# Two more seven-product chunks per layer, combined in PSUM with ScalarE copies, and input sums taken from the transposes' banks

## The chip, the cores and the metric

The kernel runs on one core of one Trainium2 chip. The engines that matter are TensorE (PE in the profile; PEld is its weight load), VectorE (DVE), ScalarE (ACT) and GpSimd (POOL, which also issues some DMAs); SyncE (SP) issues the others. PE writes only into PSUM, which has eight banks of 128 partitions by 512 fp32 numbers; DVE and ACT read and write PSUM and SBUF. The metric is the device time of one execution in microseconds (us), the median of three runs.

## What is computed

A trunk of two layers over a residual stream `h` of 512 positions by 1024 features: an attention mixer (a different one in each layer), and after each a gated feed-forward part with a causal convolution of width 3. The change touches only the feed-forward part, whose reference is:

```
def conv_ffn(xn, w_up, cw, cb, w_down):
    a = xn @ w_up                      # 512 x 1024 @ 1024 x 5632
    ap = pad(a, 2 positions in front)
    a = sum(ap[:, j:j + T] * cw[j] for j in range(3)) + cb
    gate, val = split(a, 2)            # 2816 columns each
    return (gelu(gate) * val) @ w_down # 2816 x 1024
h = h + rms_norm(mixer, g[1])
h = h + rms_norm(conv_ffn(rms_norm(h, g[2]), ...), g[3])
```

All of it is fp32. The kernel writes each factor of a matrix product as a high and a low part in PE's reduced-precision fp32 (`hi` = the rounded copy, `lo` = the value less `hi`), and makes one product from three matmuls: hi·hi, hi·lo, lo·hi (`mm3`, lines 278 to 280 before, 292 to 294 after the change; these lines are those of nearly all matmuls).

## The kernel before, in words

**Tiling.** The up-projection of a layer goes in 22 chunks. Chunk `c` is 128 gate columns and the 128 value columns that belong to them, for all 512 positions: two PSUM banks, `banks[0]` for the gate and `banks[1]` for the value, each [128 columns, 512 positions]. A bank has two halves by position, LO (0 to 255) and HI (256 to 511).

**Plain chunks** (0 to 4 and 19 to 21): for each bank 8 steps over the 1024 features, 3 matmuls of 128x512 each: 48 matmuls. Chunks 0 and 1 are woven into the end of the mixer (`first_products`).

**Seven-product chunks** (5 to 18): the two column blocks, two halves of the features and two halves of the positions make a 2x2 by 2x2 block product, which is done with seven products in place of eight (Strassen's scheme in Winograd's form). Each product has 4 steps of 3 matmuls of 128x256, so a chunk has 84 of them. The seven products need sums of weight blocks and of input blocks, and sums of the results:

- The input sums (T1 to T4, as `xsh`/`xsl` pairs in XA and XB) are made once a layer in `sums_in` (lines 671 to 690): two additions that rebuild x from its parts, one on POOL (line 675) and one on DVE, four subtractions and four splits.
- The weight sums are made for each chunk in `first_weights` and `other_weights` (lines 699 to 733), each step placed by hand among the other work with `step` and `prepare`.
- The results are combined in the chunk's banks: one ACT copy of the first product out of PSUM (`s1`, line 1020), two DVE additions into SBUF (`s12`, `s17`, lines 998 and 1001) and three in PSUM (lines 1014, 1015, 1028).

**After the products**, `taps` (lines 636 to 649) does the convolution: one ACT operation a bank and two DVE operations a bank, then `glu` (ACT, Gelu) and `product` (POOL, a multiply and a DMA of the result to HBM). The taps of chunk c run during chunk c+1.

**Weights.** `Weights` hands out raw tiles of 512 KB, loaded by SP. A pair is made by an ACT copy (hi) and then either a DVE subtraction (`low`, line 69), or an ACT copy with its sign turned and a DMA of POOL's queue that adds the raw tile onto it (`low_added`, an accumulating DMA, with no DVE work).

**The boundary ahead of the layer's chunks.** `Boundary` takes the mixer's result block by block (128 positions each): `Mix.half` squares and scales it, `norm` makes the normalised block `xn` (ACT square at line 285, ACT square root, DVE `xn` at line 295), and `transpose` has PE transpose it into two banks (`xt_ps`, line 344), from which ACT makes `xbh` (line 347) and DVE `xbl` (line 348). These run between the mixer's last matmuls and `first_products`.

**What sets the order.** The program's order on each engine is as the code is written; every engine runs its list in that order. Waits between engines are semaphore counts that the framework places from the tiles that instructions read and write. A bank of PSUM is one tile here.

Of the kernel before, what the change touches and what calls it, by code (L numbers as in the profile page):

```python
# [16 lines left out]
T = 512  # L17
# [10 lines left out]
SEVEN = (5, 6, 7, 8, 9, 10, 11, 12, 13, 14, 15, 16, 17, 18)  # L28
# [7 lines left out]
class Weights:  # L36
# [3 lines left out]
    def __init__(self, nc, new_raw, new_pair, pieces):  # L40
        self.nc, self.new_raw, self.new_pair, self.pieces = nc, new_raw, new_pair, pieces
        self.ahead, self.ahead_dma = 4, 2
        self.raw, self.ready, self.half_done = {}, {}, []
        self.kept = {}
        self.n_dma = self.n_split = self.n_get = 0
# [48 lines left out]
    def split(self, n):  # L94
        while self.n_split < min(n, len(self.pieces)):
            self.high()
# [9 lines left out]
def trunk_kernel(ctx, tc, x, norm_gains, w_qkv_a, w_o_a, w_q_b, w_o_b, kv_norm, w_kvf, b_f,  # L106
# [63 lines left out]

    dT = [tc.dram_tile([ND, 128, 2048], F32, name=f"dT{l}") for l in range(2)]

    def add_ffn(l):
        for c in range(NF):
            add_cols(w_up[l], c * 128)
            add_cols(w_up[l], DFF + c * 128)
# [41 lines left out]
    W.kept = {v0: None, v0 + 1: None}  # L218

# [119 lines left out]
    def transpose_in(b, xn, xT):  # L339

        for i in range(2):
            pt = bank([128, 4, 128], name="xt_ps")
            for k in range(4):
# [4 lines left out]
            dve.tensor_tensor(lo[:, :, s], pt, hi[:, :, s].bitcast(F32), ALU.subtract)  # L348

# [62 lines left out]
    class Boundary:  # L412
# [218 lines left out]
    def ffn(l, bd, cp, nxt, ahead):  # L631
# [4 lines left out]
        def taps(c, banks, between=None):  # L636
            bb = t4([128, 2, T], name="bb")
            for s, ch in ((0, c), (1, NF + c)):
                ps = banks[s]
                act.activation(bb[:, s, :], ps, AF.Identity, bias=cp[:, 3, ch:ch + 1], scale=cp[:, 2, ch:ch + 1])  # L640
                dve.scalar_tensor_tensor(bb[:, s, 1:], ps[:, :T - 1], cp[:, 1, ch:ch + 1], bb[:, s, 1:],
                                         ALU.mult, ALU.add)
                dve.scalar_tensor_tensor(bb[:, s, 2:], ps[:, :T - 2], cp[:, 0, ch:ch + 1], bb[:, s, 2:],
                                         ALU.mult, ALU.add)
                if s == 0 and between is not None:
# [25 lines left out]
        def sums_in():  # L671

            v = [t8([128, 4, T], name=f"xsum{i}") for i in range(2)]
            for i, eng in enumerate((pool, dve)):
                eng.tensor_tensor(v[i], xT[0][i].bitcast(F32), xT[1][i].bitcast(F32), ALU.add)
            yield
            dve.tensor_tensor(v[0][:, :, LO], v[0][:, :, HI], v[0][:, :, LO], ALU.subtract)
            dve.tensor_tensor(v[0][:, :, HI], v[1][:, :, HI], v[0][:, :, HI], ALU.subtract)
            yield
            dve.tensor_tensor(v[1][:, :, HI], v[1][:, :, HI], v[0][:, :, LO], ALU.subtract)  # L680
            dve.tensor_tensor(v[1][:, :, LO], v[1][:, :, LO], v[1][:, :, HI], ALU.subtract)
            yield
            for X, src in ((XA, v[0]), (XB, v[1])):
                X += [t8([128, 4, T], F32R, name="xsh"), t8([128, 4, T], F32R, name="xsl")]
                for k in (0, 2):
                    act.copy(X[0][:, k:k + 2], src[:, k:k + 2])
                    dve.tensor_tensor(X[1][:, k:k + 2], src[:, k:k + 2], X[0][:, k:k + 2].bitcast(F32), ALU.subtract)
# [4 lines left out]
        def split_pair(pair, src, n=1024):  # L692
            act.copy(pair[:, 0, :n], src)
            yield
            dve.tensor_tensor(pair[:, 1, :n], src, pair[:, 0, :n].bitcast(F32), ALU.subtract)

        half_way = {}

        def first_weights(c):

            r0, r1 = W.take(2)
            w0, w1 = (t8([128, 2, 1024], F32R, name="w") for _ in range(2))
# [1263 lines left out]
```

## Time and profile before

The median of three runs is 1098.94 us (1098.63 to 1099.54). The profiled execution has a span of 1096.9 us from the first to the last instruction; 2.0 us of the median lie outside it.

| engine | busy us | share | instructions |
|---|---|---|---|
| PE | 1088.0 | 99% | 6896 |
| PEld | 956.4 | 87% | 6896 |
| DVE | 923.2 | 84% | 1534 |
| ACT | 687.4 | 63% | 1164 |
| POOL | 299.8 | 27% | 393 |

Where the layers lie in the span (from the start of the matmuls of each stage):

| stage | layer 0 | layer 1 |
|---|---|---|
| first products (chunks 0, 1) | 177.05 | 754.36 |
| chunks 2 to 4 (plain) | 201.80 | 779.11 |
| chunks 5 to 18 (seven products) | 234.47 | 811.78 |

How to read it: the profile's lines give a line of the code, the engine, the operation, the tile written and the tiles read, and times in us. A matmul's listed duration is longer than the distance to the next one, since matmuls are pipelined; the distance between starts is what it costs PE.

### The profile page before, as it was taken

The numbers are of one execution on the slowest core, as the hardware profiler recorded it, in microseconds if no ns is written. First come the engines' busy times: TensorE is split into PE (matmuls) and PEld (weight loads), VectorE is DVE, ScalarE is ACT, GpSimd is POOL, SyncE is SP. The second block draws the span as 40 slices with busy tenths as digits, with TensorE's granted clock in tenths as the row PEclk, the third lists the DMA queues.
The fourth block names the chain that finished last, engine by engine and source line by source line (L and its number), as shares of the span: only waits on it lengthen the run. The fifth ranks groups of instructions, "written<-read, shape, count | busy, mean of one in ns | idle before, by whom it ended". The sixth has DMA issues, their size and how long they took to land.

```text
span 1096.9 us, 19014 instructions
## 1 busy us (share of the span) xinstructions
PE 1088.0 (99%) x6896; PEld 956.4 (87%) x6896; DVE 923.2 (84%) x1534; ACT 687.4 (63%) x1164; POOL 299.8 (27%) x393
## 2 busy tenths in 40 slices
PE   9999999999999999999999999999999999999997
PEld 6988889899999988887988788789889999988886
DVE  6677778989999799897877877958989999799994
ACT  6644565567767547576565677756567677547572
POOL 4632101223233232000010667600223333231000
PEclk9999999999999999999999999999999999999999
DMA  9579854478999999794872777574378989999872
GB/s 315 141 272 407 334 154 137 106 153 205 214 205 211 267 339 345 275 327 95 212 154 77 213 230 202 164 235 130 92 164 200 211 205 212 270 339 339 291 249 77
DMA packets 188102, 240.52 MB, mean 219 GB/s; under 512 B 12193, under 2 KB 131993, under 8 KB 187497
## 3 DMA queue, kind: packets, MB, share of 16 engines
q1 hardware_dynamic: 167848, 177.66, 50.2%
q0 software_dynamic: 20160, 61.65, 25.2%
q8 instruction: 54, 0.88, 0.3%
q14 instruction: 40, 0.32, 0.1%
HBM read 170.28 MB, written 39.63 MB: 191 GB/s over the span
## 4 chain that ended last, share of the span: by engine, by line
PE 87%; issue 6%; DMA 2%; ACT 2%; DVE 1%; POOL 1%; SPq 0%; DVEq 0%; POOLq 0%; ACTq 0%
PE up L279 13%; PE up L278 13%; PE up L280 13%; PE acc L278 8%; PE acc L280 8%; PE acc L279 8%; PE qk_ps L1299 2%; PE o_ps L1818 2%; PE pT_ps L1803 2%; PE first L278 1%; PE first L280 1%; PE first L279 1%; PE qk_ps L278 1%; PE s_ps L1771 1%; PE qk_ps L280 1%
## 5 line engine op out<-in xcount | busy, mean ns | idle before, releaser
L278 PE MATMUL up<-xsh,w 128*128 128x256 f32 x448 | 126.9, 283 | 0.0
L280 PE MATMUL up<-xsh,w 128*128 128x256 f32 x448 | 126.9, 283 | 0.0
L279 PE MATMUL up<-xsl,w 128*128 128x256 f32 x448 | 126.9, 283 | 0.0
L278 PE MATMUL acc<-w 128*128 128x512 f32 (+1 forms) x311 | 120.6, 388 | 0.0
L280 PE MATMUL acc<-w 128*128 128x512 f32 (+1 forms) x311 | 120.4, 387 | 0.0
L640 ACT ACTIVATE bb<-up,conv 128x512 f32<-128x512 f32 x80 | 59.2, 775 | 92.3 <-DVE w L716 46.0
L279 PE MATMUL acc<-w 128*128 128x512 f32 (+1 forms) x267 | 103.3, 387 | 0.0
L69 DVE TENSOR_TENSOR w<-wraw,w 128x1024 fp32r<-128x1024 f32 x66 | 89.0, 1370 | 12.7 <-ACT w L60 12.3
L60 ACT CAST w<-wraw 128x1024 fp32r<-128x1024 f32 x80 | 82.3, 1050 | 9.3 <-issue 3.8
L280 PEld LDWEIGHTS up<-xsh,w 128*128 128x128 f32 x448 | 86.1, 192 | 0.0
L278 PEld LDWEIGHTS up<-xsh,w 128*128 128x128 f32 x448 | 86.1, 192 | 0.0
L279 PEld LDWEIGHTS up<-xsl,w 128*128 128x128 f32 x448 | 86.1, 192 | 0.0
L279 PE MATMUL up<-xcl,w 128*128 128x256 f32 (+1 forms) x264 | 85.0, 322 | 0.0
L279 PE MATMUL up<-xbl,w 128*128 128x256 f32 (+1 forms) x264 | 85.0, 322 | 0.0
L278 PE MATMUL up<-xbh,w 128*128 128x256 f32 (+1 forms) x264 | 85.0, 322 | 0.0
L278 PE MATMUL up<-xch,w 128*128 128x256 f32 (+1 forms) x264 | 85.0, 322 | 0.0
L280 PE MATMUL up<-xch,w 128*128 128x256 f32 (+1 forms) x264 | 85.0, 322 | 0.0
L280 PE MATMUL up<-xbh,w 128*128 128x256 f32 (+1 forms) x264 | 85.0, 322 | 0.0
L656 POOL TENSOR_TENSOR hc<-bb 128x512 f32<-128x512 f32 x44 | 68.6, 1559 | 27.0 <-ACT bb L661 13.6
L727 POOL DMA_DIRECT2D w<-wraw x28 | 24.0, 856 | 186.0 <-ACT w L726 178.8
L278 PEld LDWEIGHTS acc<-w 128*128 128x128 f32 x311 | 58.4, 188 | 11.9
L280 PEld LDWEIGHTS acc<-w 128*128 128x128 f32 x311 | 58.4, 188 | 11.8
(337 smaller groups left out, 3340.8 us busy)
## 6 DMA issues: line engine op xcount, KB each, us to landing
wraw<-in_w_up_dram SPq DMA_DIRECT2D x88, 512.0 KB, 6.4
w<-wraw POOLq DMA_DIRECT2D x42, 512.0 KB, 6.0
dT<-dsums SPq DMA_DIRECT2D x26, 512.0 KB, 4.1
hD<-hc POOLq DMA_DIRECT2D x44, 256.0 KB, 3.8
dact<-hD SPq DMA_DIRECT2D x44, 256.0 KB, 5.9
wraw<-dT SPq DMA_DIRECT2D x22, 512.0 KB, 6.8
wraw<-in_w_down_dram SPq DMA_DIRECT2D x22, 512.0 KB
dsums<-in_w_down_dram SPq DMA_DIRECT2D x18, 512.0 KB, 8.4
```

Of the source, the lines that this page charges most:

```text
L60: self.nc.scalar.copy(pair[:, 0, s], raw[:, s])
L69: self.nc.vector.tensor_tensor(pair[:, 1, s], raw[:, s], pair[:, 0, s].bitcast(F32), ALU.subtract)
L278: pe.matmul(o, ah, bh, start=first, stop=False, skip_group_check=shared)
L279: pe.matmul(o, ah, bl, start=False, stop=False, skip_group_check=shared)
L280: pe.matmul(o, al, bh, start=False, stop=last, skip_group_check=shared)
L640: act.activation(bb[:, s, :], ps, AF.Identity, bias=cp[:, 3, ch:ch + 1], scale=cp[:, 2, ch:ch + 1])
L656: pool.tensor_tensor(hc[c], bb[:, 0, :], bb[:, 1, :], ALU.mult)
L727: pool.dma_start(w3[:, 1, 0:512], a22, accum_op=ALU.add)
L1299: pe.matmul(o, ax(0, b, kc)[x], w[:, k, :], start=kc == 0 and x == 0 and w is wh, stop=kc == KD - 1 and w is wl)
L1771: pe.matmul(s[i][hh][:, :nn], q[a][rows, qs], k[b][rows, :nn], start=n == 0, stop=n == 2)
L1803: pe.transpose(o[:, k0 + k, :], p[:, hh, k * 128:(k + 1) * 128], ident)
L1818: pe.matmul(o[64 * hh:64 * hh + 64, i * 128:(i + 1) * 128], Vt[hd // 8][:, k, (hd % 8) * 64:(hd % 8) * 64 + 64], pT[j, i, hh][:, k, :], st ...
```

## The change

SEVEN becomes 3 to 18, so chunks 3 and 4 of each layer are made by seven products. Four things go with it.

1. *Combination.* A chunk's products come in the order S2, S3, A12, S1, then A11 of the next chunk, then A22, S4 (before: S2, S3, S1, A22, A11 of the next, A12, S4). Three ACT copies take results out of PSUM (`s1`, `u2`, `s7`; lines 999, 1023, 1028) and three DVE additions work in PSUM (lines 1035, 1038, 1049). The two additions into SBUF are gone.
2. *Weight sums.* `seven_weights` makes the blocks in another form: A11 as its own small pair (`wa`, 512 columns), A12 and A22 as one pair with one accumulating DMA, and the sums with a broadcast addition of 1024 columns (line 740) and two subtractions of 512 columns (lines 739, 745), two of them in place in the raw tile. Raw tiles are loaded by two DMAs of 256 KB.
3. *Input sums.* For blocks 0 and 1, ACT copies the transposes' banks into `xlow` (line 464). For blocks 2 and 3, DVE subtracts out of the banks (lines 468, 469). `sums` has two more DVE subtractions. `sums_in`, its POOL addition among it, is gone. `split_sums` makes the pairs.
4. *Taps and the first weights.* `taps` does the second bank first, and the DVE operations in another order. The weights of chunks 0 to 2 take the accumulating DMA in place of DVE's subtraction (`W.added`).

The core of the diff:

```diff
-SEVEN = (5, 6, 7, 8, 9, 10, 11, 12, 13, 14, 15, 16, 17, 18)
+SEVEN = tuple(range(3, 19))
...
     def split(self, n):
         while self.n_split < min(n, len(self.pieces)):
+            if self.n_split in self.added:
+                self.high_added()
+                continue
             self.high()
             self.low()
...
+    W.added = {n + i for n in starts for i in range(2 * SEVEN[0])}
...
         def transpose(self, b):
             if self.xT is None:
                 self.xT = new_xT(self.name)
-            transpose_in(b, self.xn.pop(b), self.xT)
+                self.low = t8([128, 2, 4, 256], name="xlow")
+            pts = transpose_in(b, self.xn.pop(b), self.xT)
+            s = slice(b % 2 * 128, b % 2 * 128 + 128)
+            if b < 2:
+                for i, pt in enumerate(pts):
+                    act.copy(self.low[:, i, :, s], pt)
+                return
+            if b == 2:
+                self.high = t8([128, 2, 4, 256], name="xsum")
+            dve.tensor_tensor(self.high[:, 0, :, s], pts[0], self.low[:, 0, :, s], ALU.subtract)
+            dve.tensor_tensor(self.high[:, 1, :, s], pts[1], self.high[:, 0, :, s], ALU.subtract)
...
+        def seven_weights(c):
+            r0, r1 = W.take(2)
+            a = t8([128, 2, 512], F32R, name="wa")
+            act.copy(a[:, 0], r0[:, 0:512])
             yield
+            act.activation(a[:, 1], r0[:, 0:512], AF.Copy, scale=-1.0)
+            pool.dma_start(a[:, 1], r0[:, 0:512], accum_op=ALU.add)
+            yield
+            b = t8([128, 2, 1024], F32R, name="w")
+            act.copy(b[:, 0], r1)
+            yield
+            act.activation(b[:, 1], r1, AF.Copy, scale=-1.0)
+            pool.dma_start(b[:, 1], r1, accum_op=ALU.add)
...
+            sb = t4([128, 1024], name="wsum")
+            dve.tensor_tensor(r0[:, 0:512], r0[:, 512:1024], r0[:, 0:512], ALU.subtract)
+            dve.tensor_tensor(sb.rearrange("p (q c) -> p q c", q=2), r0.rearrange("p (q c) -> p q c", q=2),
+                              r1[:, None, 512:1024].to_broadcast([128, 2, 512]), ALU.add)
+            u = t8([128, 2, 1024], F32R, name="w")
+            act.copy(u[:, 0], sb)
             yield
+            dve.tensor_tensor(r0[:, 512:1024], r1[:, 0:512], sb[:, 0:512], ALU.subtract)
+            v = t8([128, 2, 1024], F32R, name="w")
+            act.copy(v[:, 0], r0)
...
+            dve.tensor_tensor(u[:, 1], sb, u[:, 0].bitcast(F32), ALU.subtract)
...
+            dve.tensor_tensor(v[:, 1], r0, v[:, 0].bitcast(F32), ALU.subtract)
...
-                prod(o2, w["S2"], (*XB, HI))
-                prod(o3, w["S3"], (*XA, HI), True)
...
-                prod(o2, w["S1"], (*XA, LO))
-                prod(o3, w["A22"], (*XB, LO))
-                dve.tensor_tensor(o4, o2, s17, ALU.add)
-                dve.tensor_tensor(o3, o3, s12, ALU.add)
+                prod(o2, w.pop("S2"), (*XB, HI))
+                prod(o3, w.pop("S3"), (*XA, HI), True)
+                product()
+                bb = taps(*before)
...
+                act.copy(u2, o2)
...
+                prod(o1, w.pop("A12"), x21)
+                prod(o2, w.pop("S1"), (*XA, LO))
+                act.copy(s7, o3)
                 glu(before[0], bb)
...
+                dve.tensor_tensor(o1, o1, s1, ALU.add)
+                if m in SEVEN:
+                    step(m)
+                dve.tensor_tensor(o4, o2, s7, ALU.add)
+                if m in SEVEN:
+                    step(m)
+                    opened = open_seven(m)
...
-                prod(o1, w["A12"], x21)
-                prod(o2, w["S4"], x22)
+                prod(o3, w.pop("A22"), (*XB, LO))
                 prepare(c, 1)
+                dve.tensor_tensor(o3, o3, u2, ALU.add)
+                prod(o2, w.pop("S4"), x22)
                 prepare(c, 2)
-                dve.tensor_tensor(o2, o2, s1, ALU.add)
```

Here `o1`, `o2` are the LO and HI halves of `banks[0]`, `o3`, `o4` those of `banks[1]`; `m` is c+1 and `n` is c+2.

The order on PE in chunk 7 of layer 0 before, the first matmul of each product (`up_2725` and `up_2726` are the chunk's two banks, `up_2855` the first bank of chunk 8; `xsh` are the input sums, `xbh` the input itself; in brackets the engines whose counts the instruction waits for):

```order
L278 MATMUL up_2725<-xsh_2380,w_2548 128x256 [waits Activation_49]
...
L278 MATMUL up_2726<-xsh_2297,w_2548 128x256
...
L278 MATMUL up_2725<-xsh_2297,w_2712 128x256 [waits DVE_49,Activation_49]
...
L278 MATMUL up_2726<-xsh_2380,w_2713 128x256 [waits DVE_49]
...
L278 MATMUL up_2855<-xbh0_1854,w_2673 128x256
...
L278 MATMUL up_2725<-xbh1_1855,w_2547 128x256 [waits DVE_49]
...
L278 MATMUL up_2725<-xbh1_1855,w_2712 128x256
```

These are S2, S3, S1, A22, A11 of chunk 8, A12, S4. S1's DVE count is that of the addition at line 998, A22's that of line 1001, and A12's that of line 1014, which reads `up_2725`.

The same place of the changed kernel (`up_2854` and `up_2855` are the banks of chunk 7, `up_2984` the first of chunk 8):

```order
L292 MATMUL up_2854<-xsh_2265,w_2843 128x256 [waits Activation_49]
...
L292 MATMUL up_2855<-xsh_2290,w_2846 128x256 [waits PE_49]
...
L292 MATMUL up_2854<-xbh1_1859,w_2718 128x256 [waits Activation_49]
...
L292 MATMUL up_2854<-xsh_2290,w_2843 128x256
...
L292 MATMUL up_2984<-xbh0_1858,wa_2809 128x256
...
L292 MATMUL up_2855<-xsh_2265,w_2718 128x256 [waits DVE_49,Activation_49]
...
L292 MATMUL up_2854<-xbh1_1859,w_2846 128x256
```

These are S2, S3, A12, S1, A11 of chunk 8, A22, S4. S2 waits for the ACT copy `s1` (line 999), A12 for the ACT copy `u2` (line 1023). A22, which writes the LO half of `up_2855`, now waits for the ACT copy `s7` (line 1028) and for a DVE count that is that of line 1038, the addition `o4` into the HI half of `up_2855`.

The order on DVE in one chunk of the changed kernel, up to the next chunk's first weight sum:

```order
L739 TENSOR_TENSOR wraw<-wraw 128x512 [waits DMAHW1_49,DMAHW0_49,DMASW1_49]
L740 TENSOR_TENSOR wsum<-wraw 128x1024 [waits DMAHW3_49,DVE_49]
L745 TENSOR_TENSOR wraw<-wraw,wsum 128x512 [waits DMAHW2_49,DVE_49]
L1035 TENSOR_TENSOR up<-up,csum 128x256 [waits PE_49]
L752 TENSOR_TENSOR w<-wsum,w 128x1024 [waits DMASW4_49,Activation_49]
L1038 TENSOR_TENSOR up<-up,csum 128x256 [waits DVE_49]
L755 TENSOR_TENSOR w<-wraw,w 128x1024 [waits Activation_49]
L1049 TENSOR_TENSOR up<-up,csum 128x256 [waits DVE_49,PE_49]
L676 SCALAR_TENSOR_TENSOR bb<-up,conv,bb 128x511 [waits Activation_49] x2
L676 SCALAR_TENSOR_TENSOR bb<-up,conv,bb 128x510 [waits DVE_49] x2
```

The additions in PSUM are the rows `up<-up,csum`: `o1` (line 1035), `o4` (1038), `o3` (1049), with the low parts of the next chunk's weight sums (752, 755) between them. The wait of line 1035 on PE is for the last matmul of S1, which writes the other half of the same bank. Before, the additions of lines 1014 and 1015 stood back to back behind the taps.

The order on ACT at the boundary of the changed kernel, from block 0's transposes to the square of block 1's norm; before, line 299's square (285 there) came right behind the two casts:

```order
L363 CAST xbh_1858<-xt_ps 128x4x128 [waits PE_49]
L363 CAST xbh_1859<-xt_ps 128x4x128 [waits PE_49]
L464 COPY xlow<-xt_ps 128x4x128 [waits DVE_49] x2
L299 ACTIVATE junk,s_1879<-h 128x1024
L301 ACTIVATE sd<-s_1879,eps_t 128x1 [waits Activation_49]
```

The DVE count that the two copies wait for is that of the subtractions `xbl` (line 364) from the same two banks.

More of the change, by code (lines that the diff above doesn't have):

```diff
@@ L732, in other_weights @@
[L732 to L733 removed]
+            dve.tensor_tensor(u[:, 1], sb, u[:, 0].bitcast(F32), ALU.subtract)
+            del u, sb
+            yield
+            dve.tensor_tensor(v[:, 1], r0, v[:, 0].bitcast(F32), ALU.subtract)
         def plain_weights(c):
@@ L963, in ffn @@
         next(extra)
+        step(S0, 1)
         post(1, first[2:4])
+        del first
         next(extra)
-        W.ahead = 1
-        W.split(base + 8)
+        next(extra)
+        next(extra, None)
+        step(S0, 1)
         begun = opened = None
```

184 lines of the change are left out of this document (82 added, 102 removed).

## The prediction

> **What bounds the kernel now.** I read the page's busy shares first, then a table of windows over the up-projections, then the timelines of PE, DVE and ACT in one chunk.
>
> ```profile
> PE 1088.0 (99%) x6896; PEld 956.4 (87%) x6896; DVE 923.2 (84%) x1534; ACT 687.4 (63%) x1164; POOL 299.8 (27%) x393
> 234.00:435.00 201.00, 201.00 (x1441) 190.69 (x1440) 181.99 (x271) 132.33 (x176) 65.59 (x78) 1.00 0.93 248
> 812.00:1012.00 200.00, 200.00 (x1437) 189.85 (x1436) 181.45 (x270) 132.17 (x175) 65.69 (x78) 1.00 0.92 249
> 201.80:234.40 32.60, 32.60 (x146) 27.02 (x145) 30.17 (x33) 22.58 (x27) 8.01 (x9) 1.00 0.63 137
> ```
>
> The columns of the windows are span, then busy time of PE, PEld, DVE, ACT and POOL, the granted clock, the DMA share and GB/s. PE is busy for all of each window at a granted clock of 1.00: in the stage that is changed no engine ever keeps PE waiting. So PE's own work is the bound, less PE work is a gain one for one, and any new wait in PE's list is a loss one for one. DVE is the next engine (181.99 of 201 us): there is little slack to hide a late DVE operation.
>
> **What the change takes off PE.** A matmul costs the distance between starts:
>
> ```profile
> 203.19 0.39 PE L278 MATMUL up<-xbh,w 128*128 128x512 f32 x1
> ...
> 203.87 0.39 PE L278 MATMUL up<-xbh,w 128*128 128x512 f32 x1
> ...
> 334.90 0.28 PE L278 MATMUL up<-xbh,w 128*128 128x256 f32 x1
> ...
> 336.10 0.28 PE L279 MATMUL up<-xbl,w 128*128 128x256 f32 x1
> ```
>
> The first row stands three matmuls ahead of the second, the third ten ahead of the fourth: 0.68 / 3 = 0.2267 us for 512 columns, 1.20 / 10 = 0.120 for 256. A plain chunk is 48 x 0.2267 = 10.88 us, one of seven products 84 x 0.120 = 10.08. Two chunks more in each of two layers: 4 x 0.80 = **3.2 us less**. That is all the change can win, since DVE and ACT work that it removes (the POOL addition, two DVE additions a chunk) stands beside a PE that does not wait.
>
> **What it adds in each chunk: a wait of A22.** In the list of PE, A22 now waits for the DVE addition of line 1038 (`o4`), because both write the same bank, though different halves. In DVE's list `o4` stands behind `o1` (line 1035) and the low part of a weight sum (line 752), and `o1` waits for the last matmul of S1. On PE only A11 of the next chunk stands between S1 and A22. So I lay this chain end to end from rows of one chunk:
>
> ```profile
> 333.70 0.28 PE L280 MATMUL up<-xbh,w 128*128 128x256 f32 x1
> 334.02 0.37 ACT L1020 COPY csum<-up 128x256 f32<-128x256 f32 x1 [0.62 <-PE up L280]
> 336.91 0.42 DVE L1028 TENSOR_TENSOR up<-up,csum 128x256 f32<-128x256 f32 x1
> 337.25 1.22 DVE L716 TENSOR_TENSOR w<-wsum,w 128x1024 fp32r<-128x1024 f32 x1
> 338.38 0.42 DVE L998 TENSOR_TENSOR csum<-up,csum 128x256 f32<-128x256 f32 x1
> 215.04 0.75 DVE L643 SCALAR_TENSOR_TENSOR bb<-up,conv,bb 128x510 f32<-128x510 f32 x1
> 215.88 0.63 ACT L661 ACTIVATE bb<-bb 128x512 f32<-128x512 f32 x1 [2.19 <-DVE bb L643]
> ```
>
> From the start of a product's last matmul (333.70) to the start of the reader that waits for it (334.02) are 0.32 us. An addition in PSUM takes DVE 0.34 to the next start (336.91 to 337.25) and 0.42 to its end; a low part of 1024 columns takes 1.13 to the next start (337.25 to 338.38). From the end of a DVE operation (215.04 + 0.75 = 215.79) to an engine waiting for it are 0.09. With S1's first matmul at T: its last starts at T + 11 x 0.12 = T + 1.32; `o1` starts at T + 1.64; line 752 at T + 1.98; `o4` at T + 3.11, and ends at T + 3.53; A22 may start at T + 3.62. PE is ready for it at T + 2 x 12 x 0.12 = T + 2.88. **PE stalls 0.74 us in each chunk**, and the period goes from 10.08 to 10.82, nearly that of a plain chunk. The low part finds its high part ready: ACT has for one chunk about 7.5 us of work by the rows below, and stands idle before S1 ends. Chunk 18 is free of it: a plain chunk follows, no weight sum stands before `o4`, and the 12 matmuls of 512 columns that take A11's place last 2.72 us. So 15 chunks a layer, the first of which comes under the start-up; 2 x 14 x 0.74 = **20.7 us more**.
>
> DVE's own sum does not bind in this stage: per chunk the change needs two additions less and some 8.5 us by these rows. It is the place of one operation, not the load.
>
> ```profile
> L641 DVE SCALAR_TENSOR_TENSOR bb<-up,conv,bb 128x511 f32<-128x511 f32 x24 | 17.8, 742 | 0.8 <-DMA dsums<-in_w_down_dram 0.8
> L640 ACT ACTIVATE bb<-up,conv 128x512 f32<-128x512 f32 x22 | 16.2, 774 | 30.8 <-DVE w L716 11.5 <-PE up L280 10.5 <-DVE up L1028 8.8
> L729 ACT CAST w<-wsum 128x1024 fp32r<-128x1024 f32 x7 | 7.4, 1053 | 0.0
> L726 ACT ACTIVATE w<-wraw 128x512 fp32r<-128x512 f32 x7 | 4.4, 635 | 0.0
> ```
>
> [...]
>
> **What it adds at the boundary.** ACT's two copies into `xlow` for blocks 0 and 1 stand ahead of the next block's square, and each waits for the subtraction `xbl` from its bank.
>
> ```profile
> 167.88 1.07 ACT L347 CAST xbh<-xt_ps 128x512 fp32r<-128x512 f32 x2
> 168.82 1.08 ACT L285 ACTIVATE junk<-h 128x1024 bf16<-128x1024 f32 x1
> 168.73 1.28 DVE L348 TENSOR_TENSOR xbl<-xt_ps,xbh 128x512 fp32r<-128x512 f32 x2
> 170.55 1.42 DVE L295 SCALAR_TENSOR_TENSOR xn<-h,rs,gain 128x512 f32<-128x512 f32 x2
> 173.43 1.03 PE L344 MATMUL xt_ps<-ident,xn 128*128 128x128 f32 x8
> 175.02 1.28 DVE L348 TENSOR_TENSOR xbl<-xt_ps,xbh 128x512 fp32r<-128x512 f32 x2
> 176.89 1.42 DVE L295 SCALAR_TENSOR_TENSOR xn<-h,rs,gain 128x512 f32<-128x512 f32 x2
> 179.92 1.04 PE L344 MATMUL xt_ps<-ident,xn 128*128 128x128 f32 x8
> ```
>
> `xbl` ends at 170.01; the second copy runs from 170.1 for about 0.55 (half of the pair of casts). The square then starts at 170.55 or so, not at 168.82: 1.7 later, and `xn` ends at 171.97 + 1.7 = 173.67, where its transposes stood at 173.43. Stall 0.3 with the release. In the next round DVE's list has slipped by 1.7, its `xbl` by 1.2, and the copies take 1.7 again: `xn` ends 2.9 later, at 181.2, against 179.92 + 0.3: stall 1.0. Together **1.3 us a layer, 2.7 in all**. Bounds: 0 if the two copies hide in the 1.5 us between `xn` and its transposes, 2 a layer if DVE slips more.
>
> **What it adds at the start-up.** Chunk 3 is now the first of seven products, and its preparation stands at the place where chunks 0 and 1 have their taps. DVE's first weight sum (line 739) overwrites the raw tile, so it waits for the accumulating DMA that reads it.
>
> ```profile
> w<-wraw POOLq DMA_DIRECT2D x28, 256.0 KB, 3.7
> 188.14 1.06 ACT L60 CAST w<-wraw 128x1024 fp32r<-128x1024 f32 x1
> 193.43 0.78 ACT L640 ACTIVATE bb<-first,conv 128x512 f32<-128x512 f32 x1 [4.23 <-PE first L280]
> 197.99 1.28 ACT L661 ACT_TABLE_LOAD   x1 [0.97 <-DVE bb L643]
> 189.23 5.04 DVE L69 TENSOR_TENSOR w<-wraw,w 128x1024 fp32r<-128x1024 f32 x1
> 188.57 4.62 POOL L675 TENSOR_TENSOR xsum<-xbh,xbl 128x2048 f32<-128x2048 f32 x1 [51.77 <-DVE xbl L348]
> ```
>
> From 188.1 ACT makes the copies of a plain piece (1.05, 1.06) and those of A11 of chunk 3 (0.61, 0.64): 191.2. With 0.3 for the issue and 3.7 to 4 to land, line 739 starts at about 195.6. Now the engines wait for each other in turn: three DVE sums, ACT's highs of u and v (to 199.6) and of T2 (200.6), and only then the taps of chunk 0, which stood at 193.43. DVE's taps end at 204.5, the table load and Gelu at 206.4, T4's high at 207.3, its low at 209.2 (beside POOL's multiply: the row of 5.04 us, against 1.22, shows a DVE operation of two SBUF inputs held for as long as POOL's runs), u's low at 210.3, the taps of chunk 1 at 212.9, its Gelu at 213.6, T3's and T1's highs at 215.5, the lows of T3, T1 and v at 218.1. PE would start S2 of chunk 3 at 201.80 + 10.88 + 1.44 = 214.1. It waits there for ACT's copy `s1`, queued behind T1's high, until 215.9: 1.7 us; at S3 for v's low: 0.6; at A12 for the copy `u2`, which stands behind eight operations of ACT: 1.9; and at A22 for `o4`: 1.6. **5.6 us a layer** (5.8 with, 5.2 without the hold by POOL), and by 5.5 us to land 7.3; 11.2 in all. Below: some 3 if the queue's distances are shorter than I laid them.
>
> **What costs nothing.** The SP loads as two DMAs of 256 KB have a chunk of slack. The accumulating DMAs for chunks 0 to 2 take DVE work away and land some 10 us before PE needs them; uncovered, each would cost its 6.0 us of landing less what remains. The tail behind chunk 18 and the down-projection are as before.
>
> **Sum.** -3.2 + 20.7 + 2.7 + 11.2 = +31.4 us: a span of 1128.3, and with the 2.0 us that lie between the profiled span and the median of the runs, **1130 us**, 2.9% slower.
>
> **The rivals.** (1) *The waits are hidden and only PE's work counts*: 1098.9 - 3.2 = 1095.7, faster. For it: DVE is idle 8% of the stage, and a PSUM addition is short. Against it: the order of the lists is fixed, and `o4` would have to end 0.74 us earlier with its low part standing ahead. It decides if `o4` is done by T + 2.8. (2) *Only the start-up and boundary cost; A22's wait is met in the steady chunk*: 1098.9 - 3.2 + 13.9 = 1109.6. For it: the chain has only 0.74 us to lose, and the 1.13 of the low part is most of it. Against it: the four terms of the chain are measured at equal shapes. (3) *The waits go by halves*: then S4 is the one to wait for `o4`, 1.44 us later, the stall is gone, the `xlow` copies run beside `xbl`, and the start-up costs about 1 us a layer: 1098.9 - 3.2 + 2 = 1097.7, no change within what can be told. Against it: the program's counts. (4) *The loss feeds itself*: ACT's queue slips so that u's high or `u2` comes late in every chunk, or the landings of the accumulating DMAs (6.0 us median for 512 KB) reach A12's low matmul, at 0.3 to 1 us a chunk: 28 x 0.3 to 28 x 1 on top, 1139 to 1158. For it: DMAs are busy 93% of the stage; against it: PE's longer period gives them more room.
>
> **How the numbers follow.** The forecast has 0.63, its own range 1121 to 1139 (start-up from 3 to 7.3 and boundary from 0 to 2 a layer, the chunk from 0.6 to 0.8). Rival 2 has 0.13, rival 4 0.16, rival 1 0.05, rival 3 0.03. The range that leaves out 2 in 10 at most takes in the upper part of rival 2 and the lower of rival 4: 1110 to 1146. No change means within 0.2%, 2.2 us. Faster is rival 1 and a part of rival 3: 0.05; same 0.03; slower 0.92.
>
> **What would show it.** The distance from one chunk's first matmul to the next's is 10.8 us, with one gap of 0.7 ahead of A22's first matmul, released by DVE line 1038; a busy PE of 93% in the window of the chunks. In chunk 3 four gaps (S2, S3, A12, A22) with 5 to 6 us together; ahead of `first` two gaps at the transposes. DVE's `o1` starts 0.32 behind S1's last matmul. Wrong would be: no gap at A22, a gap in another place (S4, or A12 behind `u2` in every chunk), or a start-up over 8 us a layer.

## The result, and the profile after

The changed kernel takes 1144.24 us (median of four runs, 1144.14 to 1145.52), the one before 1098.79: 4.1% slower, ratio 1.0411 (95% interval 1.0397 to 1.0426). The profiled execution has a span of 1142.2 us, 45.3 more than before. The forecast was 1130: right in sign and in the place of the main loss, 14 us too low.

The page's busy shares, and two windows of layer 0 (span, then busy time of PE, PEld, DVE, ACT, POOL, the granted clock, DMA share, GB/s), the chunks from 4 on and the place of chunk 3:

```profile
PE 1098.7 (96%) x7040; PEld 964.8 (84%) x7040; DVE 878.4 (77%) x1468; ACT 735.8 (64%) x1264; POOL 301.6 (26%) x407
236.00:390.00 154.00, 144.95 (x1182) 142.36 (x1181) 123.12 (x169) 112.47 (x167) 49.48 (x56) 1.00 0.77 189
203.00:236.00 33.00, 28.13 (x170) 25.69 (x169) 23.80 (x30) 23.25 (x34) 8.38 (x9) 0.90 0.53 125
```

PE waits now in a stage where it never did: 9 of 154 us in the first window. DVE's busy time has fallen from 923.2 to 878.4 us, as the change meant, and experiment 8 shows that this is worth nothing. In the second window the granted clock is 0.90, where the windows of before that the prediction shows have 1.00.

One chunk of the steady stretch, first PE around A22 of one chunk and the start of the next one's, then DVE and ACT:

```profile
284.13 0.28 PE L294 MATMUL up<-xbh,wa 128*128 128x256 f32 x1
285.06 0.36 PE L292 MATMUL up<-xsh,w 128*128 128x256 f32 x1 [0.65 <-ACT w L729]
285.25 0.28 PE L293 MATMUL up<-xsl,w 128*128 128x256 f32 x1
296.00 0.36 PE L292 MATMUL up<-xsh,w 128*128 128x256 f32 x1 [0.65 <-ACT w L729]
283.01 0.43 DVE L1035 TENSOR_TENSOR up<-up,csum 128x256 f32<-128x256 f32 x1 [0.30 <-PE up L294]
283.36 1.22 DVE L752 TENSOR_TENSOR w<-wsum,w 128x1024 fp32r<-128x1024 f32 x1
284.49 0.43 DVE L1038 TENSOR_TENSOR up<-up,csum 128x256 f32<-128x256 f32 x1
283.93 1.04 ACT L729 CAST w<-wraw 128x1024 fp32r<-128x1024 f32 x1
```

The chain of the prediction stands there as it was laid: `o1` (L1035) behind S1, the low part (L752), `o4` (L1038) until 284.92, A22 at 285.06. A22 comes 0.93 us behind the matmul before it, not 0.12: a gap of 0.81. Its first matmul takes 0.19 to the next start (285.06 to 285.25), 0.07 more than the others. From one A22 to the next are 10.94 us here and 10.95 in the mean of chunks 4 to 17: 0.87 over the 84 x 0.120 = 10.08.

The profile names an ACT operation (L729, a weight copy for a later chunk) as what released A22. It ended at 284.97, by chance just behind `o4`; it is not what A22 needs. (At A22 of chunk 3, at 230.31, the profile names line 1038 itself.) The first experiment shows which it was.

The start of chunk 3, on PE, DVE and ACT, and the windows of what follows:

```profile
215.28 0.39 PE L294 MATMUL up<-xbh,w 128*128 128x512 f32 x1
219.29 0.58 PE L292 MATMUL up<-xsh,w 128*128 128x256 f32 x1 [3.62 <-ACT csum L999]
219.67 0.42 PE L293 MATMUL up<-xsl,w 128*128 128x256 f32 x1
219.89 0.41 PE L294 MATMUL up<-xsh,w 128*128 128x256 f32 x1
199.31 0.69 DVE L739 TENSOR_TENSOR wraw<-wraw 128x512 f32<-128x512 f32 x1 [5.17 <-issue]
218.88 0.36 ACT L999 COPY csum<-up 128x256 f32<-128x256 f32 x1
...
219.29:224.58 5.29, 5.29 (x24) 5.29 (x25) 3.96 (x5) 5.29 (x9) 2.96 (x4) 0.50 0.44 80
224.58:228.78 4.20, 4.20 (x36) 4.20 (x36) 4.08 (x7) 2.49 (x5) 1.44 (x3) 1.00 1.01 211
819.00:821.92 2.92, 2.92 (x13) 2.92 (x14) 2.25 (x2) 2.92 (x5) 0.87 (x1) 0.50 0.09 15
```

PE waits 3.8 us ahead of S2, not 1.7, and then runs at a granted clock of 0.50 for 5.29 us (24 matmuls, about 0.22 apart in place of 0.12) in layer 0 and for 2.92 us in layer 1. S3 and A12, which were to wait 0.6 and 1.9, come that much later in layer 0 and find their operands there; in layer 1, with 13 slow matmuls, A12 still waits for `u2`.

Two places more lose time where the forecast had none. Ahead of the down-projection's first products (`acc`):

```profile
431.43 0.39 PE L292 MATMUL acc<-w 128*128 128x512 f32 x1
433.52 0.50 PE L293 MATMUL acc<-w 128*128 128x512 f32 x1 [1.71 <-DVE w L815]
429.78 1.42 DVE L676 SCALAR_TENSOR_TENSOR bb<-up,conv,bb 128x511 f32<-128x511 f32 x2 [3.56 <-ACT bb L673]
431.12 1.21 DVE L815 TENSOR_TENSOR w<-dact,w 128x1024 fp32r<-128x1024 f32 x1
432.25 2.35 DVE L815 TENSOR_TENSOR w<-wraw,w 128x1024 fp32r<-128x1024 f32 x2
434.52 1.40 DVE L676 SCALAR_TENSOR_TENSOR bb<-up,conv,bb 128x510 f32<-128x510 f32 x2
```

and at chunks 18 and 19 (gaps of 0.2 and 0.6 us in layer 0), of which the second waits for a landing:

```profile
393.47 0.50 PE L294 MATMUL up<-xbh,w 128*128 128x512 f32 x1 [0.32 <-DMA w<-wraw]
```

From the starts of the matmuls of each stage, both kernels side by side, the 45.3 us go here (the stages outside the feed-forward parts differ by 0.5 us the other way):

| place | forecast, us | measured, us | from |
|---|---|---|---|
| PE's own work | -3.2 | -3.2 | counts and distances as before |
| A22, chunks 4 to 17, both layers | +20.7 | +24.4 | 28 x (10.95 - 10.08) |
| boundary, both layers | +2.7 | +1.9 | first products to chunk 2: 25.71 and 25.69, before 24.75 |
| start-up, chunk 3 | +11.2 | +15.5 | layer 0: 3.83 at S2, 2.41 of slow matmuls, 1.49 at A22; layer 1: 3.93, 1.37, 0.92 at A12, 1.60 at A22 |
| chunks 18 and 19 | 0 | +1.8 | gaps, with the longer first matmuls |
| start of the down-projection | 0 | +5.4 | to the next transposes: 103.36 and 103.37, before 100.65 and 100.64 |
| sum | +31.4 | +45.8 | |

### The profile page after: what moved, and what is told of

It is laid out like the page before. It is cut to its first block, busy times and chain, and to the rows that moved or that the text cites. A ratio compares the mean times of both kernels' runs of the same rounds, so it can differ in the third digit from the quotient of the medians.

```text
span 1142.2 us, 19621 instructions
## 1 busy us (share of the span) xinstructions
PE 1098.7 (96%) x7040; PEld 964.8 (84%) x7040; DVE 878.4 (77%) x1468; ACT 735.8 (64%) x1264; POOL 301.6 (26%) x407
## 4 chain that ended last, share of the span: by engine, by line
PE 64%; DVE 13%; ACT 12%; issue 7%; DMA 3%; POOL 0%; SPq 0%; DVEq 0%; ACTq 0%; POOLq 0%
PE acc L293 7%; PE acc L294 7%; PE acc L292 7%; PE up L292 5%; PE up L294 5%; PE up L293 4%; DVE bb L676 4%; DVE wsum L740 3%; ACT w L747 2%; ACT w L729 2%; PE v_ps L292 2%; PE v_ps L293 2%; PE v_ps L294 2%; ACT bb L673 2%; PE qk_ps L1325 2%
## 5 line engine op out<-in xcount | busy, mean ns | idle before, releaser
L292 PE MATMUL up<-xsh,w 128*128 128x256 f32 x512 | 149.2, 291 | 28.1 <-ACT w L729 16.8
L676 DVE SCALAR_TENSOR_TENSOR bb<-up,conv,bb 128x511 f32<-128x511 f32 (+1 forms) x160 | 112.0, 745 | 47.5 <-ACT bb L673 47.4
L293 PE MATMUL up<-xsl,w 128*128 128x256 f32 x512 | 146.3, 286 | 0.0
L294 PE MATMUL up<-xsh,w 128*128 128x256 f32 x512 | 146.3, 286 | 0.0
L292 PEld LDWEIGHTS up<-xsh,w 128*128 128x128 f32 x512 | 99.6, 195 | 34.5 <-ACT w L729 21.3
L293 PEld LDWEIGHTS up<-xsl,w 128*128 128x128 f32 x512 | 99.8, 195 | 0.1
L294 PEld LDWEIGHTS up<-xsh,w 128*128 128x128 f32 x512 | 99.7, 195 | 0.0
L673 ACT ACTIVATE bb<-up,conv 128x512 f32<-128x512 f32 x80 | 61.1, 777 | 55.4 <-DVE up L1049 41.1
L69 DVE TENSOR_TENSOR w<-wraw,w 128x1024 fp32r<-128x1024 f32 x50 | 61.5, 1246 | 14.1 <-ACT w L60 12.3
L292 PEld LDWEIGHTS acc<-w 128*128 128x128 f32 x311 | 58.4, 188 | 12.0
L294 PEld LDWEIGHTS acc<-w 128*128 128x128 f32 x311 | 58.4, 188 | 11.6
L293 PEld LDWEIGHTS acc<-w 128*128 128x128 f32 x267 | 50.1, 188 | 16.2 <-DVE w L815 6.2
L292 PE MATMUL up<-xch,w 128*128 128x256 f32 (+1 forms) x192 | 61.3, 319 | 0.7 <-ACT csum L1023 0.7
L294 PE MATMUL up<-xch,w 128*128 128x256 f32 (+1 forms) x192 | 61.2, 319 | 0.5 <-DMA w<-wraw 0.5
L743 ACT CAST w<-wsum 128x1024 fp32r<-128x1024 f32 x32 | 33.6, 1050 | 43.6 <-DVE wsum L740 43.6
L294 PE MATMUL up<-xbh,w 128*128 128x256 f32 (+1 forms) x192 | 61.2, 319 | 0.3 <-DMA w<-wraw 0.3
```

The costliest lines, as they stand in the source:

```text
L69: self.nc.vector.tensor_tensor(pair[:, 1, s], raw[:, s], pair[:, 0, s].bitcast(F32), ALU.subtract)
L292: pe.matmul(o, ah, bh, start=first, stop=False, skip_group_check=shared)
L293: pe.matmul(o, ah, bl, start=False, stop=False, skip_group_check=shared)
L294: pe.matmul(o, al, bh, start=False, stop=last, skip_group_check=shared)
L673: act.activation(bb[:, i, :], ps, AF.Identity, bias=cp[:, 3, ch:ch + 1], scale=cp[:, 2, ch:ch + 1])
L676: dve.scalar_tensor_tensor(bb[:, i, n:], ps[:, :T - n], cp[:, 2 - n, ch:ch + 1], bb[:, i, n:], ALU.mult, ALU.add)
```

## Experiments

### 1. Is it o4's place? Directly behind o1

```diff
                 dve.tensor_tensor(o1, o1, s1, ALU.add)
+                dve.tensor_tensor(o4, o2, s7, ALU.add)
                 if m in SEVEN:
                     step(m)
-                dve.tensor_tensor(o4, o2, s7, ALU.add)
```

> The addition o4 stands directly behind o1 in VectorE's list, ahead of the low part of the next chunk's weight sum; nothing else is changed. Theory (o4 is late only because the low part of 1024 columns stands ahead of it): o4 ends 1.13 us earlier, 0.3 us ahead of the time at which PE is ready for A22; the gap of 0.81 us ahead of A22 and the slower first matmul behind it are gone in chunks 4 to 17, the chunks come every 10.08 us, and 28 x 0.87 = 24 us go: 1120 us (1117 to 1123). Rival (A22 is held by something else in the chunk: ScalarE's copy s7, the weight pair that the released row names, or VectorE's load as a whole): the gap stays at 0.8 us and the time at 1144, within 3 us.

Measured: 1120.79 us (four runs, 1118.32 to 1123.45), ratio to before 1.0203 (1.0184 to 1.0223); 23.5 us less than the change by the medians. DVE, and the window of the same chunks:

```profile
280.45 0.43 DVE L1035 TENSOR_TENSOR up<-up,csum 128x256 f32<-128x256 f32 x1 [0.28 <-PE up L294]
280.99 0.43 DVE L1036 TENSOR_TENSOR up<-up,csum 128x256 f32<-128x256 f32 x1
281.33 1.22 DVE L752 TENSOR_TENSOR w<-wsum,w 128x1024 fp32r<-128x1024 f32 x1
...
232.00:370.00 138.00, 138.00 (x1152) 138.00 (x1151) 119.65 (x165) 107.95 (x164) 48.71 (x55) 1.00 0.85 209
```

PE is busy for all of 138 us: no gap is left in the steady chunks. The order of two DVE operations was worth the whole steady loss, and the ACT copy that the profile named as the releaser is where it was. By the starts of the matmuls in the two profiles, chunks 4 to 17 take 24.2 us less and chunk 3 takes 2.3 less; chunks 18 and 19 take 1.9 more, and the start of the down-projection 1.3 more, where eight matmuls of layer 0 run at the half clock. So a part of what was gained came back as longer waits further on, and the total meets the expected one partly because these cancel.

### 2. The other way: o4 behind both low parts

```diff
                 if m in SEVEN:
                     step(m)
-                dve.tensor_tensor(o4, o2, s7, ALU.add)
                 if m in SEVEN:
                     step(m)
+                dve.tensor_tensor(o4, o2, s7, ALU.add)
+                if m in SEVEN:
                     opened = open_seven(m)
```

> The addition o4 stands one operation further back, behind both low parts. Theory: the gap ahead of A22 grows by the 1.13 us that the second low part takes on VectorE, to 1.9 us, in every chunk from 3 to 17: 30 x 1.13 = 34 us more, 1178 us (1174 to 1182). Rival (o4 does not decide A22's start): 1144 us, within 3 us.

Measured: 1224.81 us (one run), 43 us above the expected range. The gap is as long as expected, the time is not:

```profile
258.58 0.28 PE L294 MATMUL up<-xbh,wa 128*128 128x256 f32 x1
260.65 0.36 PE L292 MATMUL up<-xsh,w 128*128 128x256 f32 x1 [1.78 <-ACT w L731]
260.84 0.28 PE L293 MATMUL up<-xsl,w 128*128 128x256 f32 x1
261.29 0.42 PE L293 MATMUL up<-xsl,w 128*128 128x256 f32 x1
261.50 0.42 PE L294 MATMUL up<-xsh,w 128*128 128x256 f32 x1
258.94 1.22 DVE L755 TENSOR_TENSOR w<-wraw,w 128x1024 fp32r<-128x1024 f32 x1
260.07 0.43 DVE L1040 TENSOR_TENSOR up<-up,csum 128x256 f32<-128x256 f32 x1
261.00:264.40 3.40, 3.40 (x19) 3.40 (x18) 0.43 (x1) 0.64 (x1) 2.59 (x3) 0.51 1.11 261
264.40:272.10 7.70, 7.70 (x66) 7.70 (x65) 6.40 (x9) 5.29 (x10) 0.86 (x1) 0.99 0.37 85
```

The gap is 2.07 - 0.12 = 1.95 us, 1.13 more than in the change: the length of one low part (L755), behind which `o4` (L1040 there) now stands. But behind it the granted clock falls to a half, 0.51 for 3.4 us here, and over the chunks from 250 to 420 us it is 0.88 in the mean, some 41 us of half clock in 12 or 13 chunks: 16 matmuls at 0.213 in each. That is 16 x 0.093 = 1.5 us a chunk more, and 30 x (1.13 + 1.5) = 79 us against the 80.6 measured. `o4` decides when A22 starts, as expected; the theory had left out that PE runs at half pace behind a gap of this length here.

### 3. How long may a gap be?

```diff
+                for _ in range(2):
+                    dve.tensor_tensor(s1, s1, s1, ALU.add)
                 dve.tensor_tensor(o4, o2, s7, ALU.add)
```

The two additions overwrite `s1` behind its last use; no result is changed.

> Two additions of 256 columns within SBUF, whose result nobody uses, stand on VectorE between the low part and o4: o4 ends 0.8 us later, and the gap ahead of A22 goes from 0.81 to 1.6 us in every chunk, where it was 1.94 with o4 behind both low parts. Theory (the half pace of 16 matmuls behind each gap of 1.94 us needs a gap of some length, and the single gaps of 1.4 to 1.5 us in chunk 3 did not bring it): no slow matmuls in chunks 4 to 17, 30 x 0.8 = 24 us more, 1168 us (1164 to 1172). Rival (each gap over about 1 us that comes every 11 to 13 us brings it): 16 matmuls at 0.21 us behind the gaps, 28 x 1.5 = 42 us more still, 1205 to 1212 us.

Measured: 1167.02 us (one run). The gap is 1.60 us in each chunk, and the matmuls behind it run 0.12 apart:

```profile
235.00:370.00 135.00, 119.14 (x975) 117.23 (x973) 109.81 (x161) 92.67 (x140) 39.67 (x45) 1.00 0.72 176
```

So 28 gaps of 1.60 us cost their own length, 28 of 1.95 us cost nearly double. From 1.87 to 2.34 us the length alone does not decide: in this kernel's chunk 3 a gap of 1.93 us (layer 0) has 16 slow matmuls behind it and one of 2.34 (layer 1) none, and the same gap of 1.87 us ahead of the down-projection has none in the changed kernel and eight slow matmuls in layer 0 of experiment 1. The two gaps of over 3 us in the changed kernel (3.83 and 3.93) have 24 and 13 slow matmuls behind them.

The trace of the changed kernel shows where the clock changes: at 217.75, 224.58, 818.50, 821.91 and 1139.35 us, 2, 174, 1 and 93 times 3.413 us apart. So I read the idle time of PE by stretches of 3.41 us. Here are those around the two gaps of chunk 3 of this experiment, layer 0 and then layer 1:

```profile
227.63:231.04 3.41, 1.64 (x15) 1.46 (x14) 3.38 (x5) 3.07 (x4) 0.04 (x1) 1.00 0.71 197
231.04:234.45 3.41, 3.41 (x19) 3.41 (x18) 1.24 (x3) 0.78 (x1) 2.62 (x3) 0.50 1.07 244
...
838.62:842.03 3.41, 2.16 (x18) 1.95 (x17) 3.30 (x5) 2.67 (x3) 0.00 (x0) 1.00 0.80 191
842.03:845.44 3.41, 2.49 (x21) 2.52 (x22) 2.32 (x4) 1.75 (x4) 1.62 (x2) 1.00 0.89 254
```

In layer 0 PE is idle for 3.41 - 1.64 = 1.77 us of one stretch, and the next stretch has a clock of 0.50. In layer 1 the longer gap falls into two stretches, with 1.25 and 0.92 us of idle time, and the clock stays at 1.00. The changed kernel, read the same way (the clock is the column of 1.00 and 0.50):

```profile
214.34:217.75 3.41, 1.33 (x6) 0.75 (x4) 2.03 (x4) 1.29 (x2) 0.00 (x0) 1.00 0.62 178
217.75:221.16 3.41, 1.87 (x8) 1.87 (x9) 3.10 (x3) 3.41 (x7) 0.57 (x1) 0.50 0.00 0
...
815.08:818.50 3.42, 0.19 (x1) 0.00 (x0) 1.73 (x3) 2.34 (x3) 0.00 (x0) 1.00 0.47 139
818.50:821.91 3.41, 2.92 (x13) 2.92 (x14) 2.75 (x3) 3.41 (x7) 0.87 (x1) 0.50 0.07 13
821.91:825.32 3.41, 2.75 (x23) 2.55 (x22) 2.74 (x5) 2.88 (x6) 3.14 (x4) 1.00 0.96 175
...
1030.12:1033.54 3.42, 1.71 (x9) 1.10 (x7) 3.42 (x5) 0.23 (x1) 0.00 (x0) 1.00 0.88 329
1033.54:1036.95 3.41, 3.23 (x13) 2.36 (x14) 3.34 (x6) 1.01 (x2) 0.00 (x0) 1.00 0.81 252
```

The clock is 0.50 behind the stretches with 2.08 and 3.23 us of idle time, and stays at 1.00 behind the one with 1.71, which holds the gap of 1.87 ahead of the down-projection in layer 1. These are the cases that were measured, and not a limit: at the end of the kernel before, PE is idle for the last 1.86 us of a stretch (1089.04 to 1092.45), and the clock is 1.00 in the next. By this count, which takes PE as busy to the listed end of a matmul, a gap of 1.60 us is 1.44 us idle and one of 1.95 is 1.78. That a gap acts by the stretches into which it falls is my reading of these cases; no run moved a gap against them alone.

### 4. The start-up: A11's low part of chunk 3 by DVE

```diff
-            act.activation(a[:, 1], r0[:, 0:512], AF.Copy, scale=-1.0)
-            pool.dma_start(a[:, 1], r0[:, 0:512], accum_op=ALU.add)
+            if c == SEVEN[0]:
+                dve.tensor_tensor(a[:, 1], r0[:, 0:512], a[:, 0].bitcast(F32), ALU.subtract)
+            else:
+                act.activation(a[:, 1], r0[:, 0:512], AF.Copy, scale=-1.0)
+                pool.dma_start(a[:, 1], r0[:, 0:512], accum_op=ALU.add)
```

> The low part of A11 of chunk 3 is made by VectorE and not by the accumulating DMA; the rest of the start-up is unchanged. Theory (the start-up's chain begins with the landing of that DMA, 6.4 us behind two others in its queue): the first weight sum starts some 4 us earlier, PE's gap of 3.8 us ahead of S2 of chunk 3 falls to under 0.5 us, and the 13 to 24 matmuls behind it that ran at half the pace (0.22 in place of 0.12 us) run at full pace because the gap that slowed them is gone; the later waits of chunk 3 come back in part (S3, A12, A22 together 2 to 4 us a layer). 2 x (3.8 + 1.9 + 1.5 - 3.0) = 8 us less: 1136 us (1133 to 1140). Rival 1 (ScalarE's queue, not the landing, sets the start of the chain): 1144 us. Rival 2 (the slow matmuls come from the DMA traffic or the weights of that place and not from the gap): they stay slow without the gap, 1139 to 1141 us.

Measured: 1136.90 us, ratio 1.0355 (1.0337 to 1.0372), 7.3 us less than the change. The first weight sum on DVE (L742 there), and the windows from S2 of chunk 3 on in both layers:

```profile
193.66 0.69 DVE L726 TENSOR_TENSOR wa<-wraw,wa 128x512 fp32r<-128x512 f32 x1
194.38 0.69 DVE L742 TENSOR_TENSOR wraw<-wraw 128x512 f32<-128x512 f32 x1
213.00:226.00 13.00, 10.33 (x76) 9.57 (x75) 11.43 (x14) 11.21 (x19) 4.42 (x5) 1.00 0.61 131
808.00:821.00 13.00, 10.33 (x77) 9.60 (x76) 11.55 (x14) 11.21 (x18) 4.45 (x5) 1.00 0.63 136
```

The sum starts at 194.38 and not at 199.31. S2 does not wait, no matmul is slow, and the clock is 1.00. What remains are gaps of 1.44 at A12 (for `u2`) and 1.54 at A22 (for `o4`), where the prediction had 1.9 and 1.6. Both rivals fall: the landing set the start, and the slow matmuls went with the gap.

### 5. The boundary: the copies behind the square

```diff
                 if i >= 1:
                     self.norm(self.order[i - 1])
+                if i >= 2:
+                    self.copy_low()
```

`copy_low` has the two copies into `xlow`, which are taken out of `transpose`.

> ScalarE's copies into xlow for blocks 0 and 1 stand behind the next block's square and square root, not ahead of them; nothing else is changed. Theory (these copies, each waiting for the subtraction from the same bank, delay the next block's norm): the gaps of 0.69 and 0.19 us at the transposes of block 2 (181.0 in layer 0) fall under 0.2 us together in each layer, the first products take 24.8 us in place of 25.7, 2 x 0.9 less: 1142.4 us. The time of one look can't tell this from no change; the gap can. Rival (VectorE's load in that stretch holds xn up, not the copies): the gap stays at 0.7 us.

Measured: 1143.34 us (one run), which says nothing by itself. On PE, the transposes of block 2, first of the change and then of this kernel, in layer 0:

```profile
181.00 1.29 PE L360 MATMUL xt_ps<-ident,xn 128*128 128x128 f32 x8 [0.54 <-DVE xn L309]
...
179.05 1.03 PE L360 MATMUL xt_ps<-ident,xn 128*128 128x128 f32 x8
```

The wait for `xn` is gone and the eight transposes take 1.03 as before: the copies were its cause. There is no gap of over 0.1 us left between 160 us and S2 of chunk 3.

### 6. The down-projection's gap: taps bank by bank

For chunks 19 to 21 the taps take bank 0 (both DVE operations), then the low parts, then bank 1, as before the change.

```diff
-            glu(c, taps(c, banks, between))
+            glu(c, (bank_taps if c > SEVEN[-1] else taps)(c, banks, between))
```

> The taps of chunks 19 to 21 go bank by bank again as before the change, with the low parts of the down-projection's first pieces between the two banks; chunks 0 to 18 keep the new order. Theory (in the changed order VectorE can't begin with the bank that is ready first and comes to those low parts too late): the gaps of 1.9 and 0.6 us at the down-projection's first pieces are gone in both layers, 2 x 2.7 = 5.4 us less: 1138.8 us (1137.5 to 1140.5). Rival (the gap comes from the raw tiles that land late after a longer up-projection, or from chunk 18's late end): the gap stays, 1144 us within 1.5 us.

Measured: 1138.60 us, ratio 1.0365 (1.0349 to 1.0380), 5.6 us less than the change. The low parts that PE waited for are the two rows `w<-wraw`. Against the down-projection's first matmul DVE begins them 4.0 us earlier (0.47 us ahead of it, 427.54 with 428.01; 3.54 behind it, 432.25 with 428.71, in the changed kernel), and PE's list shows no gap there:

```profile
424.27 1.53 DVE L703 SCALAR_TENSOR_TENSOR bb<-up,conv,bb 128x511 f32<-128x511 f32 x2
425.71 1.91 DVE L827 TENSOR_TENSOR w<-dact,w 128x1024 fp32r<-128x1024 f32 x1
427.54 2.35 DVE L827 TENSOR_TENSOR w<-wraw,w 128x1024 fp32r<-128x1024 f32 x2
429.81 1.52 DVE L703 SCALAR_TENSOR_TENSOR bb<-up,conv,bb 128x511 f32<-128x511 f32 x2
```

In the changed order the first DVE operations of both banks stand ahead of these low parts, and the bank that PE ends last comes first, so DVE had to wait for that bank's last matmul and for ACT's operation on it (L673; idle 3.56 us at 429.78 in the profile after).

### 7. All of it together

The edits of 1, 4, 5 and 6, and two more: the A12/A22 weights of chunk 4 are prepared behind the copy `u2` of chunk 3 and not ahead of it, and the first weights of chunk 19 half a chunk earlier, the second ones behind A22 of chunk 17. Of the diff, the two more:

```diff
+            if n == SEVEN[-1] + 1 and part == 0:
+                return
...
                 act.copy(u2, o2)
+                if c == S0:
+                    step(m, 2)
...
                 act.copy(s7, o3)
+                if n == SEVEN[-1] + 1:
+                    step(n)
...
-                    if n in SEVEN:
+                    if n in SEVEN and s == 0:
                         step(n, 2)
```

> All of it together: o4 directly behind o1; A11's low of chunk 3 by VectorE; the A12/A22 weights of chunk 4 prepared behind the copy u2 of chunk 3; late copies into xlow; taps of chunks 19 to 21 bank by bank; the first weights of chunk 19 prepared half a chunk earlier, the second ones behind A22 of chunk 17. Theory (the named waits are all that the change costs, and PE's own work then sets the time): before less the 3.2 us of PE work, and some 0.5 to 1 us of leftover waits a layer: 1097 us (1095.5 to 1099), faster than both. Rival (VectorE and ScalarE are so full that a wait taken from one place comes back at another): 1100 to 1106 us.

Measured: 1095.90 us (1095.17 to 1096.46, 11 runs) beside 1098.42 for the kernel before: ratio 0.9977 (0.9968 to 0.9986), faster than both, though only 0.2% faster than the kernel before.

```profile
PE 1085.3 (99%) x7040; PEld 960.6 (88%) x7040; DVE 883.4 (81%) x1470; ACT 732.8 (67%) x1262; POOL 301.8 (28%) x405
220.00:370.00 150.00, 149.70 (x1248) 149.50 (x1247) 129.10 (x179) 118.71 (x179) 53.19 (x60) 1.00 0.87 211
221.88 0.38 PE L292 MATMUL up<-xsh,w 128*128 128x256 f32 x1 [0.30 <-DVE up L1063]
```

One gap of 0.46 us is left in each layer, at A22 of chunk 3, again for `o4` (L1063 there). No wait came back at another place; the gaps at chunks 18 and 19 are gone too.

### 8. What the two chunks are worth

The kernel of 7 with seven products from chunk 5 on; the preparation of chunk 5 is spread over chunks 3 and 4, and the steps at the start-up and behind `u2` that prepared the first two seven-product chunks are out (not in this cut).

```diff
-SEVEN = tuple(range(3, 19))
+SEVEN = tuple(range(5, 19))
...
                     prepare(c, 1 + s)
+                    if m in SEVEN:
+                        step(m, 2)
                     if n in SEVEN:
                         step(n, 2)
```

> The kernel with all parts together, but with seven products for chunks 5 to 18 as before the change (chunks 3 and 4 plain; the preparation of chunk 5 spread over chunks 3 and 4): PE has exactly the matmuls of the kernel before. Theory (PE's work sets the time wherever no wait stands in its list, and the gain of all parts over before comes from the 4 chunks x 0.80 us alone): 3.2 us over all parts less the 0.5 us a layer that all parts still waits in chunk 3, that is the time of before, ratio 1.000 (0.998 to 1.002), 1098.4 us. Rival (the gain comes from VectorE's lighter load or the other new pieces, not from the two chunks): 1095 to 1096.5 us, as all parts together. A new wait in chunks 3 to 5 would show as a gap in PE's list and would add its length.

Measured: 1098.46 us beside 1098.67 before, ratio 0.9995 (0.9986 to 1.0004). The page's busy shares:

```profile
PE 1088.5 (99%) x6896; PEld 956.3 (87%) x6896; DVE 859.4 (78%) x1438; ACT 725.3 (66%) x1242; POOL 300.7 (27%) x405
```

With PE's matmuls as before, all the rest of the change (DVE busy for 859.4 us, before 923.2) gives no difference that can be measured. The gain of 7 is the four chunks': 0.9995 - 0.9977 = 0.0018, some 2 us, for 3.2 less the 2 x 0.56 us that chunk 3 still waits there.

## Why the prediction was right, and where it was off

The forecast's own range ended at 1139 us, 5 us below the time; only the wider range, to 1146, holds it. The terms missed by 3.7 us at A22, 4.3 at the start-up, -0.8 at the boundary and 7.2 behind the seven-product chunks: nearly all the same way, so that little cancelled.

**The steady chunk: right, size 0.74 for 0.87 us.** `o1`, the low part, `o4`, A22 stood as laid, `o4` decides (1 and 2), and the gap moves by the length of whatever stands ahead of it (1.13 in 2, 0.79 in 3). The step mis-sized was the last one, "0.09 to an engine waiting for it": from `o4`'s end (284.92) to A22 are 0.14, and the first matmul behind a wait takes 0.07 more, which the sum had left out. These are 0.12 of the 0.13 us; 28 x 0.13 = 3.7 us.

**The saving: right.** 3.2 us of PE work, seen clean only in 7 against 8.

**The start-up: right in kind, 15.5 for 11.2 us.** The step that failed is "3.7 to 4 to land": that was the median of all transfers of this size, while this one had two of 512 KB ahead of it in its queue (issued at 188.18 and 191.79). It was issued at 192.8, and line 739 started at 199.31: 6.5. In the changed kernel the same transfer took 3.3 us with nothing ahead of it (issued at 220.59) and 5.6 with two ahead (225.13), so the place in the queue fits; no run changed that place alone. The prediction's own upper case, 5.5 us, was still too short. (Its four waits also add up to 5.8 us a layer and not to the 5.6 that it carried on, which is between its two cases.) The second miss is that a wait's price was taken as its length: behind 3.8 us PE ran at a clock of 0.50, 2.41 and 1.37 us more. Where the prediction had four waits in chunk 3, the first one grew and took most of the others with it.

**The boundary: right in kind, 1.9 for 2.7 us.** The first stall (0.3) did not show; the second was 0.88 with the longer transposes, not 1.0.

**The tail: wrong.** "The tail behind chunk 18 and the down-projection are as before" was said of chunks whose matmuls had not changed. `taps` had, and with it the place of the low parts in DVE's list (6): 5.4 us. "Chunk 18 is free of it" holds for `o4`; but ACT's copies for chunk 19 (382.47 to 386.36) stood ahead of `s1` (386.27), and a DMA for chunk 19 landed late (the row at 393.47): 1.8 us.

**The rivals.** That the waits are hidden (1) and that the steady chunk is free (2) both fell with the gap of 0.81 in 28 chunks; that only halves are guarded (3) fell with it too, since S4 never waited and A22 did. The time lies in the band of the fourth, but not by its mechanism: no queue slipped from chunk to chunk, every steady chunk lost the same 0.87. (The 8% of idle DVE that it set down for the first rival is 9% by its own windows, 201 less 181.99 us, which changes nothing there.)

## What to carry to other kernels

Where PE never waits, the order of single operations on the other engines is worth more than their load: 64 us less DVE work gave nothing, and one DVE operation 1.13 us long, standing ahead of an addition that PE waits for, cost 24 us. When results are combined in PSUM, list for each write who reads or writes the same bank next (A22 here waited 0.81 us for an addition into the other half of its bank), and put that operation first in its engine's list; then look at every user of a helper whose order was changed, not only at the chunks that the change is about. The releaser that a profile row names can be a neighbour that ended at the same moment: move the suspect, and see whether the gap moves.

## What the runs showed of the hardware that was not expected

PE's granted clock was 0.50 behind some of its waits. In the changed kernel it was so for 6.83 us at the wait of 3.8 us in layer 0 (217.75 to 224.58, PE at work in the last 5.29) and for 3.41 at that of 3.9 in layer 1 (818.50 to 821.91, PE at work in 2.92); in experiment 2 for 3.4 us behind a wait of 1.95 us (0.51 from 261.00 to 264.40). Behind waits of 1.44, 1.54 and 1.60 us the clock was 1.00 (the windows of experiments 4 and 3), and from 1.87 to 2.34 us some waits had slow matmuls behind them and some had none (experiment 3). In layer 0 of the changed kernel PE was idle for 1.54 us of the first 3.41 us at half clock, and another 3.41 followed; in layer 1 it was idle for 0.49, and the clock was 1.00 behind them.

The price of a wait in the profile after is 0.32 us from the start of the last matmul of 256 columns to DVE's read (282.69 to 283.01, as long as in the prediction), 0.14 from DVE's end to the matmul (284.92 to 285.06), and 0.07 on that matmul (0.19 to the next start in place of 0.12).
